# A mixer's second output projection by a seven-product scheme, behind each two gate pairs

## The chip, the cores and the metric

The kernel runs on one core of one Trainium2 chip. The metric is the device time of one execution in microseconds (us): the median of several runs. Engines are named as the profile names them: PE is TensorE (matmuls), PEld its weight loads, DVE is VectorE, ACT is ScalarE, POOL is GpSimd, SP is SyncE, which here only issues transfers.

## The reference

Two layers (DEPTH = 2) of a streaming encoder, on 640 tokens: 512 of a new stream and 8 x 16 of running streams. Everything is float32.

```python
x += 1/2 * SwiGLU_1(RMSNorm(x))
h  = RMSNorm(x)
z  = h @ w_in              # conv B | conv C | conv V | q | k | v | gates
y_conv = B * causal_depthwise_conv3(C * V)          # 512 channels
y_attn = chunk-band attention, 8 heads x 64         # 512 channels
g_conv, g_attn = split(sigmoid(gates + b_gate))     # 1024 columns each
m  = g_conv * (y_conv @ w_conv_out) + g_attn * (y_attn @ w_attn_out)
x += m @ w_o
x += 1/2 * SwiGLU_2(RMSNorm(x))
```

`w_conv_out` and `w_attn_out` are 512 x 1024, `w_o` is 1024 x 1024.

## The kernel before

**Layout.** Channels lie on the 128 partitions, the 640 tokens (T) along the free dimension, in two halves of 320 (HT, called t1 and t2). A row of 1024 outputs is KT = 8 tiles of 128; the inputs of `w_attn_out` are CT = 4 tiles.

**Precision.** Each float32 operand is split into a high part (a rounded copy, made by ScalarE, L306 for weights) and a low part (operand minus high part, made by VectorE, L311). A product is three matmuls: high x high, high weight x low input, low weight x high input (`multiply`, `block`).

**Weights** come from one stream in HBM in transfers of 128 x 1024 (`raw`, three buffers, issued by SP at L246). A slab is what one step of TensorE uses; `prep` casts it and leaves its low part in `pending`, `flush` makes the low parts. `slab(True)` hands out the next slab, after it has put the cast of the slab two further on into ScalarE's order. The high and low parts have three buffers each.

**By seven.** Some products are done as a 2 x 2 block product with seven block products in place of eight (Winograd's form of Strassen's scheme). Tokens are cut into halves and inputs into even and odd tiles. A group of output tiles needs sums of weights (VectorE, L250, four half-slabs a group), sums of inputs (made once), and seven blocks of 12 matmuls of 320 columns, in four slabs: slab 0 gives blocks one and two, slab 1 three and four, slab 2 five and six, slab 3 the seventh. Several blocks add onto one PSUM bank; between them the bank's content is copied out, since the intermediate values are needed too.

**The output stage** (`outputs`, in each layer after attention) has its order written out by hand: PE, DVE and ACT run their instructions strictly in the order in which the program gives them. It goes through:

- `gate_pair(m)` for m = 2 to 14, two gate tiles at a time, by seven over the normalised input `h` (called g2, g4, ... here). It has banks pa, pb and pc. In pairs 2, 4 and 6 the intermediate products are copied to SBUF (L1300) and added by POOL's accumulating transfers (`accumulate`, L1280); in pairs 8 to 14, marked `direct`, VectorE adds them from PSUM (`take`).
- `unit(m0, to)` for m0 = 0 and 4: four output tiles of `w_conv_out` by seven, over the input sums `xhi`/`xlo` made of `yc`. Banks A, B and two of C.
- `out(m)`, two after each of pairs 8 to 14: one output tile of `w_attn_out` as a plain product (`product`, L373): 4 input tiles x 3 matmuls x 2 halves. The parts of `yas`, the attention's output, are made by `taken` (L1483) and `took` (L1490). Then the product is multiplied with its gate (L1468) and added to `mm`.
- Small pieces of VectorE's and ScalarE's work are put at four spots of each pair or unit with `at(place, spot, job)`: `scale` (times the norm's factors, L1283), `bend` (two sigmoids, L1125), `weigh` (`mm` times its gate).
- `give` splits the merged rows `mm` into the operands `mo` of `w_o` (L220, L221), most of them during the last two `out`s.

Then `mixer` does the eight rows of `w_o`, one after the other, each a plain product over the eight operands (bank `po`), adds each to `x` (L1206) and prepares the next block's inputs.

Of the kernel before, what the change touches and what calls it, by code (L numbers as in the profile page):

```python
# [108 lines left out]
def mixer_order():  # L109

    mix = lambda *rows: ("mix", rows)
    out = [("v", None)] + [mix(("q", p), ("k", p)) for p in range(AW // P)]
    for c in range(0, CT, 2):
        out += [mix(("C", c + i), ("V", c + i)) for i in range(2)] + [mix(("B", c), ("B", c + 1))]
    gates = [mix(("g", m), ("g", m + 1)) for m in range(0, 2 * KT, 2)]
    out += gates[:4] + [("unit", ("co", 0)), ("unit", ("co", 4))]
    for i, g in enumerate(gates[4:]):
        out += [g, ("ao", 2 * i), ("ao", 2 * i + 1)]  # L120
    return out + [("o", m) for m in range(KT)]


# [58 lines left out]
def trunk(ctx: ExitStack, tc: tile.TileContext, xin, wst, small, pbias, samplebias, kcache, vcache,  # L182
# [24 lines left out]
    def acc(name):  # L207
        return banks["acc"].tile([P, 2, 512], F32, tag="acc", name=name)
# [40 lines left out]
    def add(out, a, b):  # L249
        DVE.tensor_tensor(out=out, in0=a, in1=b, op=ALU.add)  # L250
# [135 lines left out]
    def product(ps, ops, at=()):  # L386
        for _ in steps(ps, ops, at):
            pass
# [718 lines left out]
    def mixer(l, after):  # L1107
# [91 lines left out]
        ex = after()  # L1199
        with tc.manual_schedule(engines=ORDERED):  # L1200
            hold[0] = True
            for m in range(KT):
                po = acc(f"po{l}_{m}")
                product(po, mo)
                ex.weights(m)
                DVE.tensor_tensor(out=halves(x[m]), in0=two(po), in1=halves(x[m]), op=ALU.add)  # L1206
                if m < KT - 1:
                    flush()
                ex.final(m)
# [51 lines left out]
    def outputs(l, gp, X, st, cs, yc, yas, sigmoid, gates):  # L1261
# [20 lines left out]
        def times(out, g):  # L1282
            DVE.tensor_tensor(out=out, in0=out, in1=g, op=ALU.mult)  # L1283

        def gate_pair(m):
            n = f"{l}_{m}"
            pa, pb, pc = (att(f"q{i}{n}")[:, :HT] for i in "abc")
            direct = m >= KT
            if m in (4, 6):
                u, g = (gp.tile([P, T], F32, name=f"g{n}{i}") for i in "ab")  # L1290
            else:
                u, g = tmp(f"g{n}"), tmp(f"g{n}_1")
            gates[m], gates[m + 1] = u, g
            me = f"g{m}"

            def take(out, ps, c):
                if direct:
                    add(out, ps, out)
                else:
                    ACT.copy(c, ps)  # L1300
                    accumulate(out, c)

            s0 = quiet()
            block(pa, s0, 0, x11, every, True, True)
            ACT.copy(u[:, t1], pa)
            prep(used[0] + 1)
            flush()
            spot(me, 1)
            block(pb, s0, 1, x21, every, True, True)
            if direct:  # L1310
                take(u[:, t1], pb, cs[0])
# [9 lines left out]
            if not direct:  # L1321
                take(u[:, t1], pb, cs[0])
# [7 lines left out]
            if direct:  # L1330
                times(g[:, t2], rr[:, t2])
                times(u, rr)
                sigmoid(u, m)
            block(pa, s3, 0, xT4, every, False, True)
            DVE.tensor_tensor(out=g[:, t1], in0=pa, in1=rr[:, t1], op=ALU.mult)
            if direct:
                sigmoid(g, m + 1, -1.0)
            flush()
            spot(me, 4)

# [6 lines left out]
        def bend(m):  # L1347
            def job():
# [1 line left out]
                sigmoid(gates[m + 1], m + 1, -1.0)  # L1350
            return job

        v = yc.rearrange("p (i o) (t c) -> p i o t c", o=2, t=2)
# [3 lines left out]
        vs = [v[:, i].rearrange("p o t c -> p (o t) c") for i in range(2)]  # L1357

        def high(i, c, z):
            ACT.copy(xhi[:, i, c], z)  # L1360
# [1 line left out]
        def low(i, c, z):  # L1362
            DVE.tensor_tensor(out=xlo[:, i, c], in0=z, in1=xhi[:, i, c].bitcast(F32), op=ALU.subtract)

        def opening():
            high(slice(0, 2), 4, v[:, :, 0, 0])
            for i in range(2):
                high(i, slice(5, 7), v[:, i, 1])

        def firsts():  # L1370
            low(slice(0, 2), 4, v[:, :, 0, 0])
            DVE.tensor_tensor(out=v[:, :, 0, 0], in0=v[:, :, 0, 0], in1=v[:, :, 0, 1], op=ALU.subtract)

        def lasts():
            DVE.tensor_tensor(out=v[:, :, 0, 1], in0=v[:, :, 1, 1], in1=v[:, :, 0, 1], op=ALU.subtract)
            for a, b in ((v[:, :, 0, 0], v[:, :, 1, 1]), (v[:, :, 1, 1], v[:, :, 1, 0])):
                DVE.scalar_tensor_tensor(out=b, in0=a, scalar=-1.0, in1=b, op0=ALU.mult, op1=ALU.subtract)

        def raw_low(i):
            return lambda: low(i, slice(5, 7), v[:, i, 1])  # L1380

        def sum_high(i):
            return lambda: high(i, slice(0, 4), vs[i])

        def sum_low(i):
            return lambda: low(i, slice(0, 4), vs[i])

        def unit(m0, to):

            n = f"{l}_{m0}"  # L1390
            A, B = (acc(f"{i}co{n}") for i in ("ba" if m0 else "ab"))
            if m0:
                A, B = B, A
            C = [att(f"c{i}co{n}")[:, :HT] for i in range(2)]
            a, b = ([z[:, i, :HT] for i in range(2)] for z in (A, B))
            me = f"c{m0}"

            def mul(ps, s, half, kind, start):
                for i in range(2):
# [51 lines left out]
                    times(mm[m], gates[m])  # L1451
            return job

        def parts(pool, tag, name, src):
            hi, lo = (pool.tile([P, T], F32R, tag=f"{tag}{i}", name=f"{name}{i}") for i in ("hi", "lo"))
            split(hi, lo, src)
            return hi, lo

        ya, mo = [], []

        def out(m, then=None):

            py = acc(f"py{l}_{m}")
            product(py, ya)
            if then:
                then()
            g = gates[m + KT]
            DVE.tensor_tensor(out=halves(g), in0=two(py), in1=halves(g), op=ALU.mult)  # L1468
            add(mm[m], mm[m], g)
            flush()  # L1470

        def give(ms):
            for m in ms:
                mo.append(parts(hp, "h", f"m{l}_{m}", mm[m]))

        for c in range(CT):
            ya.append(tuple(z[:, c // 2, :].rearrange("p a b -> p (a b)")[:, (c % 2) * T : (c % 2 + 1) * T]
                            for z in (xhi, xlo)))

        def taken(*cs):  # L1480
            def job():
                for c in cs:
                    ACT.copy(ya[c][0], yas[:, c, :])  # L1483
            return job

        def took(*cs):
            def job():
                for c in cs:
                    hi, lo = ya[c]
                    DVE.tensor_tensor(out=lo, in0=yas[:, c, :], in1=hi.bitcast(F32), op=ALU.subtract)  # L1490
            return job

        at("g2", 1, opening)
        at("g2", 2, firsts)
        at("g2", 3, raw_low(0))
        at("g2", 4, raw_low(1))
        at("g4", 1, lasts)
        at("g4", 3, sum_high(0))
        at("g4", 4, sum_high(1))
        at("g6", 1, sum_low(0))  # L1500
        at("g6", 2, sum_low(1))
        at("g6", 3, scale(2))
        at("g6", 4, bend(2))
        at("c0", 1, scale(4))
        at("c0", 2, bend(4))
        at("c0", 3, scale(6))
        at("c0", 4, bend(6))
        at("c4", 2, weigh(0, 1))
        at("c4", 4, weigh(2, 3))
        at(f"g{KT}", 1, taken(0, 1))  # L1510
        at(f"g{KT}", 2, took(0, 1), taken(2, 3))
        at(f"g{KT}", 3, took(2, 3))
        at(f"g{KT + 2}", 2, weigh(5, 7))
        at(f"g{KT + 2}", 4, weigh(4, 6))
        for m in (2, 4, 6):
            gate_pair(m)
        unit(0, yc)
        unit(CT, spare)
# [566 lines left out]
```

## Time and profile before

| | |
|---|---|
| median of 3 runs | 2506.02 us (2505.72 to 2506.08) |
| profiled execution | 2506.0 us, span from first to last instruction 2504.2 us |
| PE busy | 2486.0 us, 99% of the span, 17096 matmuls |
| DVE busy | 2104.6 us, 84% |
| ACT busy | 1420.0 us, 57% |
| POOL busy | 335.6 us, 13% |
| mean granted TensorE clock | 0.998 of full |
| transfers | 299.59 MB, mean 120 GB/s |

Busy time of PE counts pipelined matmuls from start to end; what bounds a stage is read from the starts. A row of the timeline has the start, the duration, the engine, the line, the operation, output<-inputs by the program's names, shapes and a count; in square brackets stands the idle time before it and who ended it. Rows of groups have the count, the busy time and the mean duration.

### The profile page before, as it was taken

To read this page: it belongs to the slowest core of one execution; us is meant where nothing else is said; L and a number is where in the kernel's file an instruction comes from. 1 tells how busy PE (TensorE), PEld (TensorE's weight loads), DVE (VectorE), ACT (ScalarE), POOL (GpSimd) and SP (SyncE) were. 2 spreads that over 40 slices of the span, in tenths; PEclk is the share of its full clock that TensorE was granted. 3 is DMA by queue.
4 is the path that set the end of the run, shared out by engine and by line. 5 is a ranking of instruction groups with operands and counts; after the bars stand their busy time and mean duration, and the time that the engine had idled before them with its cause. 6 is when DMAs were issued, how large, how long until landed. Compare 5 with 4: busy or idle time off the path is not lost. (4 is left out here: it accounts for less than half of the span.)

```text
span 2504.2 us, 43427 instructions
## 1 busy us (share of the span) xinstructions
PE 2486.0 (99%) x17096; PEld 2427.1 (97%) x17096; DVE 2104.6 (84%) x3304; ACT 1420.0 (57%) x2281; POOL 335.6 (13%) x407
## 2 busy tenths in 40 slices
PE   9999999999999999999999999999999999999998
PEld 8999999888999999999999999998899999999998
DVE  7888888878886899888788889888788868989887
ACT  7455556665654555555555555556646455555554
POOL 0011211211100011111002111221111000111111
PEclk9999999999999999999999999999999999999999
DMA  4245665335423444656435565643444243455554
GB/s 145 81 110 123 138 137 130 108 105 173 108 73 107 101 116 116 137 134 135 116 87 128 129 133 122 137 119 117 133 143 108 77 114 94 119 132 120 131 135 110
DMA packets 127021, 299.59 MB, mean 120 GB/s; under 512 B 12160, under 2 KB 70912, under 8 KB 126816
## 3 DMA queue, kind: packets, MB, share of 16 engines
q1 hardware_dynamic: 68976, 219.18, 27.6%
q0 software_dynamic: 57120, 76.98, 18.4%
q8 instruction: 134, 2.20, 0.4%
q10 hardware_dynamic: 720, 0.65, 0.1%
q14 instruction: 71, 0.58, 0.1%
HBM read 221.13 MB, written 7.94 MB: 91 GB/s over the span
## 5 line engine op out<-in xcount | busy, mean ns | idle before, releaser
L311 DVE TENSOR_TENSOR wlo<-raw,whi 128x1024 fp32r<-128x1024 f32 (+1 forms) x575 | 593.8, 1035 | 224.3 <-ACT whi L306 218.9
L306 ACT CAST whi<-raw 128x1024 fp32r<-128x1024 f32 (+1 forms) x575 | 516.0, 902 | 362.7 <-PE pbb L396 44.3
L306 ACT CAST whi<-s 128x1024 fp32r<-128x1024 f32 (+1 forms) x160 | 151.2, 945 | 249.5 <-issue 114.4
L396 PE MATMUL pab<-xhib,whi 128*128 128x320 f32 x704 | 218.2, 310 | 0.6 <-ACT ub L813 0.6
L396 PE MATMUL pab<-xhib,wlo 128*128 128x320 f32 x704 | 217.5, 309 | 0.8 <-DVE wlo L311 0.8
L396 PE MATMUL pab<-xlob,whi 128*128 128x320 f32 x704 | 217.3, 309 | 0.0
L396 PE MATMUL paa<-xhia,whi 128*128 128x320 f32 x640 | 198.0, 309 | 0.3 <-ACT ua L813 0.3
L396 PE MATMUL paa<-xhia,wlo 128*128 128x320 f32 x640 | 197.7, 309 | 0.4 <-DVE wlo L311 0.4
L396 PE MATMUL paa<-xloa,whi 128*128 128x320 f32 x640 | 197.7, 309 | 0.1
L311 DVE TENSOR_TENSOR wlo<-s,whi 128x1024 fp32r<-128x1024 f32 (+1 forms) x160 | 174.1, 1088 | 12.7 <-ACT whi L306 12.7
L396 PEld LDWEIGHTS pab<-xhib,wlo 128*128 128x128 f32 x704 | 132.1, 188 | 1.3 <-DVE wlo L311 1.3
L396 PEld LDWEIGHTS pab<-xhib,whi 128*128 128x128 f32 x704 | 132.2, 188 | 1.3 <-ACT ub L813 1.1
L396 PEld LDWEIGHTS pab<-xlob,whi 128*128 128x128 f32 x704 | 132.2, 188 | 0.2
L396 PEld LDWEIGHTS paa<-xhia,wlo 128*128 128x128 f32 x640 | 120.1, 188 | 0.7 <-DVE wlo L311 0.7
L396 PEld LDWEIGHTS paa<-xhia,whi 128*128 128x128 f32 x640 | 120.2, 188 | 0.6 <-ACT ua L813 0.6
L396 PEld LDWEIGHTS paa<-xloa,whi 128*128 128x128 f32 x640 | 120.2, 188 | 0.4 <-DVE xloa L555 0.4
L250 DVE TENSOR_TENSOR raw<-raw,raw 128x512 f32<-128x512 f32 x160 | 109.4, 684 | 1.4
L250 DVE TENSOR_TENSOR raw<-s,raw 128x512 f32<-128x512 f32 x160 | 109.8, 686 | 0.0
L396 PE MATMUL pcb<-xhib,whi 128*128 128x320 f32 x352 | 108.9, 309 | 0.4 <-ACT gb L832 0.4
L396 PE MATMUL pcb<-xhib,wlo 128*128 128x320 f32 x352 | 108.8, 309 | 0.0
L396 PE MATMUL pcb<-xlob,whi 128*128 128x320 f32 x352 | 108.6, 309 | 0.0
L979 POOL DMA_DIRECT2D x<-c_b x52 | 62.6, 1204 | 310.6 <-ACT c_b L972 134.8
(703 smaller groups left out, 8077.2 us busy)
## 6 DMA issues: line engine op xcount, KB each, us to landing
raw<-in_wst SPq DMA_DIRECT2D x375, 512.0 KB, 3.9
x<-c_b POOLq DMA_DIRECT2D x52, 320.0 KB, 5.0
x<-c_a POOLq DMA_DIRECT2D x50, 320.0 KB, 5.0
kc<-in_kcache SPq DMA_DIRECT2D x32, 256.0 KB, 3.9
vc<-in_vcache SPq DMA_DIRECT2D x16, 512.0 KB, 4.8
ub<-cbb POOLq DMA_DIRECT2D x42, 160.0 KB, 5.3
ua<-cba POOLq DMA_DIRECT2D x38, 160.0 KB, 5.2
x<-u_a POOLq DMA_DIRECT2D x18, 320.0 KB, 5.1
```

The lines of the kernel that those rows point to most:

```text
L250: DVE.tensor_tensor(out=out, in0=a, in1=b, op=ALU.add)
L306: ACT.copy(hi[:, d], src[:, c])
L311: DVE.tensor_tensor(out=lo, in0=src, in1=hi.bitcast(F32), op=ALU.subtract)
L396: PE.matmul(ps, a, b, start=start and kp == 0 and j == 0, stop=stop and kp == NP - 1 and j == 2, skip_group_check=True)
L979: POOL.dma_start(rows(r, cols), z, accum_op=ALU.add)
```

## The change

1. `w_attn_out` is done by seven as `w_conv_out` is: two units (`ao`, 0 and 4) in place of eight plain rows. They stand behind each two gate pairs: 8, 10, unit, 12, 14, unit. The host lays its weights out accordingly.
2. The sums of the attention's output that a unit needs are made in `yas` itself, in steps at spots of gate pairs 8 and 10 (class `Inputs`, used for both inputs now). The first unit writes its result over `yas`, the second into `held`, the buffer of gates 4 to 7.
3. Gate pairs 8 to 14 take the way of 2 to 6: copies by ScalarE and accumulating transfers by POOL, no `direct`.
4. Gating and merging become jobs: `join` (result times gate, added to `mm`), `give` (high part) and `gave` (low part).
5. The first two rows of `w_o` are done together, by inputs in the order 0, 1; 2, 3; 4, 6; 5, 7: both rows for each two inputs.

```diff
-    for i, g in enumerate(gates[4:]):
-        out += [g, ("ao", 2 * i), ("ao", 2 * i + 1)]
+    out += gates[4:6] + [("unit", ("ao", 0))] + gates[6:] + [("unit", ("ao", 4))]
...
+            pos = [acc(f"po{l}_{m}") for m in range(2)]
+            ws = [[tiles.take() for _ in range(KT)] for _ in pos]
+            for ks in ((0, 1), (2, 3), (4, 6), (5, 7)):
+                for po, w in zip(pos, ws):
+                    for k in ks:
+                        multiply(po, w[k], mo[k], k == 0, k == KT - 1)
             for m in range(KT):
-                po = acc(f"po{l}_{m}")
-                product(po, mo)
+                if m < len(pos):
+                    po = pos[m]
+                else:
+                    po = acc(f"po{l}_{m}")
+                    product(po, [mo[k] for k in range(KT)])
...
+        held = gp.tile([P, CT, T], F32, name=f"gt{l}")
...
             def take(out, ps, c):
-                if direct:
-                    add(out, ps, out)
-                else:
-                    ACT.copy(c, ps)
-                    accumulate(out, c)
+                ACT.copy(c, ps)
+                accumulate(out, c)
...
+        class Inputs:
+            def opening(self):
+                high(slice(0, 2), 4, self.v[:, :, 0, 0])
+                for i in range(2):
+                    high(i, slice(5, 7), self.v[:, i, 1])
+            def firsts(self):
+                v = self.v
+                low(slice(0, 2), 4, v[:, :, 0, 0])
+                DVE.tensor_tensor(out=v[:, :, 0, 0], in0=v[:, :, 0, 0], in1=v[:, :, 0, 1], op=ALU.subtract)
+            def lasts(self):
+                v = self.v
+                DVE.tensor_tensor(out=v[:, :, 0, 1], in0=v[:, :, 1, 1], in1=v[:, :, 0, 1], op=ALU.subtract)
+                for a, b in ((v[:, :, 0, 0], v[:, :, 1, 1]), (v[:, :, 1, 1], v[:, :, 1, 0])):
+                    DVE.scalar_tensor_tensor(out=b, in0=a, scalar=-1.0, in1=b, op0=ALU.mult, op1=ALU.subtract)
...
+        def join(*ms):
             def job():
+                for m in ms:
+                    times(ya[m], gates[KT + m])
+                    add(mm[m], mm[m], ya[m])
...
+        def give(*ms):
+            def job():
+                for m in ms:
+                    mo[m] = tuple(hp.tile([P, T], F32R, tag=f"h{i}", name=f"m{l}_{m}{i}") for i in ("hi", "lo"))
+                    ACT.copy(mo[m][0], mm[m])
...
+        def gave(*ms):
+            def job():
+                for m in ms:
+                    hi, lo = mo[m]
+                    DVE.tensor_tensor(out=lo, in0=mm[m], in1=hi.bitcast(F32), op=ALU.subtract)
...
-        at(f"g{KT}", 1, taken(0, 1))
-        at(f"g{KT}", 2, took(0, 1), taken(2, 3))
-        at(f"g{KT}", 3, took(2, 3))
-        at(f"g{KT + 2}", 2, weigh(5, 7))
-        at(f"g{KT + 2}", 4, weigh(4, 6))
+        at("g8", 1, second.opening)
+        at("g8", 2, second.firsts)
+        at("g8", 3, second.raw_low(0))
+        at("g8", 4, second.raw_low(1), second.lasts)
+        at("g10", 1, second.sum_high(0))
+        at("g10", 2, second.sum_high(1), second.sum_low(0))
+        at("g10", 3, second.sum_low(1))
+        at("g10", 4, scale(8))
+        at("ao0", 1, bend(8))
+        at("ao0", 2, scale(10))
+        at("ao0", 3, bend(10))
+        at("ao0", 4, join(0))
+        at("g12", 1, join(1))
+        at("g12", 2, join(2))
+        at("g12", 3, join(3))
+        at("g14", 1, scale(12))
+        at("g14", 2, bend(12), weigh(4, 5))
+        at("g14", 3, weigh(6, 7))
+        at("ao4", 1, give(0, 1))
+        at("ao4", 2, gave(0, 1))
+        at("ao4", 3, scale(14), give(2, 3))
+        at("ao4", 4, bend(14), gave(2, 3))
...
-        for m in range(0, KT, 2):
-            gate_pair(m + KT)
-            last = m == KT - 2
-            out(m, (lambda: give(range(3))) if last else None)
-            out(m + 1, (lambda: give(range(3, 6))) if last else None)
-        give(range(6, KT))
+        for m in (8, 10):
+            gate_pair(m)
+        unit("ao", 0, yas)
+        for m in (12, 14):
+            gate_pair(m)
+        unit("ao", CT, held)
+        for i, m in enumerate((4, 6, 5, 7)):
+            join(m)()
+            give(m)()
+            if i:
+                gave(was)()
+            was = m
+        gave(was)()
```

More of the change, by code (lines that the diff above doesn't have):

```diff
@@ L1287, in gate_pair @@
             pa, pb, pc = (att(f"q{i}{n}")[:, :HT] for i in "abc")
-            direct = m >= KT
             if m in (4, 6):
-                u, g = (gp.tile([P, T], F32, name=f"g{n}{i}") for i in "ab")
+                u, g = held[:, m - 4], held[:, m - 3]
             else:
@@ L1309, in gate_pair @@
             block(pb, s0, 1, x21, every, True, True)
-            if direct:
-                take(u[:, t1], pb, cs[0])
             s1 = slab(True)[0]
@@ L1320, in gate_pair @@
             spot(me, 3)
-            if not direct:
-                take(u[:, t1], pb, cs[0])
+            take(u[:, t1], pb, cs[0])
             block(pa, s2, 0, xT7, every, False, True)
@@ L1329, in gate_pair @@
             s3 = slab(True)[0]
[L1330 to L1333, printed above, removed]
             block(pa, s3, 0, xT4, every, False, True)
             DVE.tensor_tensor(out=g[:, t1], in0=pa, in1=rr[:, t1], op=ALU.mult)
-            if direct:
-                sigmoid(g, m + 1, -1.0)
             flush()
@@ L1351, in bend @@
             return job
-        v = yc.rearrange("p (i o) (t c) -> p i o t c", o=2, t=2)
         xhi, xlo = (gp.tile([P, 2, 7, HT], F32R, name=f"x{i}{l}") for i in ("hi", "lo"))
@@ L1356, in outputs @@
                  for i in range(2)]
-        vs = [v[:, i].rearrange("p o t c -> p (o t) c") for i in range(2)]
         def high(i, c, z):
@@ L1363, in low @@
             DVE.tensor_tensor(out=xlo[:, i, c], in0=z, in1=xhi[:, i, c].bitcast(F32), op=ALU.subtract)
[L1365 to L1391, printed above, removed]
+        class Inputs:
+            def __init__(self, y):
+                self.v = y.rearrange("p (i o) (t c) -> p i o t c", o=2, t=2)
+                self.vs = [self.v[:, i].rearrange("p o t c -> p (o t) c") for i in range(2)]
+            def opening(self):
[11 more added lines that the diff above has]
+                    DVE.scalar_tensor_tensor(out=b, in0=a, scalar=-1.0, in1=b, op0=ALU.mult, op1=ALU.subtract)
+            def raw_low(self, i):
+                return lambda: low(i, slice(5, 7), self.v[:, i, 1])
+            def sum_high(self, i):
+                return lambda: high(i, slice(0, 4), self.vs[i])
+            def sum_low(self, i):
+                return lambda: low(i, slice(0, 4), self.vs[i])
@@ L1392, in unit @@
+        def unit(name, m0, to):
+            n = f"{name}{l}_{m0}"
+            A, B = (acc(f"{i}{n}") for i in ("ba" if m0 else "ab"))
             if m0:
                 A, B = B, A
-            C = [att(f"c{i}co{n}")[:, :HT] for i in range(2)]
+            C = [att(f"c{i}{n}")[:, :HT] for i in range(2)]
             a, b = ([z[:, i, :HT] for i in range(2)] for z in (A, B))
-            me = f"c{m0}"
+            me = f"{name}{m0}"
             def mul(ps, s, half, kind, start):
@@ L1452, in weigh @@
             return job
[L1454 to L1480, printed above, removed]
+        def join(*ms):
             def job():
-                for c in cs:
-                    ACT.copy(ya[c][0], yas[:, c, :])
-            return job
-        def took(*cs):
+                for m in ms:
+                    times(ya[m], gates[KT + m])
+                    add(mm[m], mm[m], ya[m])
+            return job
@@ L1487, in job @@
+        mo = {}
+        def give(*ms):
             def job():
-                for c in cs:
-                    hi, lo = ya[c]
-                    DVE.tensor_tensor(out=lo, in0=yas[:, c, :], in1=hi.bitcast(F32), op=ALU.subtract)
-            return job
[L1493 to L1500, printed above, removed]
@@ L1501, in outputs @@
-        at("g6", 2, sum_low(1))
+                for m in ms:
+                    mo[m] = tuple(hp.tile([P, T], F32R, tag=f"h{i}", name=f"m{l}_{m}{i}") for i in ("hi", "lo"))
+                    ACT.copy(mo[m][0], mm[m])
+            return job
+        def gave(*ms):
[3 more added lines that the diff above has]
+                    DVE.tensor_tensor(out=lo, in0=mm[m], in1=hi.bitcast(F32), op=ALU.subtract)
+            return job
+        ya = [z[:, i] for z in (yas, held) for i in range(CT)]
@@ L1502, in outputs @@
+        first, second = Inputs(yc), Inputs(yas)
+        at("g2", 1, first.opening)
+        at("g2", 2, first.firsts)
+        at("g2", 3, first.raw_low(0))
+        at("g2", 4, first.raw_low(1))
+        at("g4", 1, first.lasts)
+        at("g4", 3, first.sum_high(0))
+        at("g4", 4, first.sum_high(1))
+        at("g6", 1, first.sum_low(0))
+        at("g6", 2, first.sum_low(1))
         at("g6", 3, scale(2))
         at("g6", 4, bend(2))
-        at("c0", 1, scale(4))
-        at("c0", 2, bend(4))
@@ L1506, in outputs @@
[L1506 to L1509, printed above, removed]
-        at(f"g{KT}", 1, taken(0, 1))
-        at(f"g{KT}", 2, took(0, 1), taken(2, 3))
-        at(f"g{KT}", 3, took(2, 3))
-        at(f"g{KT + 2}", 2, weigh(5, 7))
-        at(f"g{KT + 2}", 4, weigh(4, 6))
+        at("co0", 1, scale(4))
+        at("co0", 2, bend(4))
+        at("co0", 3, scale(6))
+        at("co0", 4, bend(6))
+        at("co4", 2, weigh(0, 1))
+        at("co4", 4, weigh(2, 3))
@@ L1515, in outputs @@
+        at("g12", 2, join(2))
[7 more added lines that the diff above has]
+        at("ao4", 4, bend(14), gave(2, 3))
         for m in (2, 4, 6):
             gate_pair(m)
-        unit(0, yc)
-        unit(CT, spare)
-        for m in range(0, KT, 2):
-            gate_pair(m + KT)
-            last = m == KT - 2
-            out(m, (lambda: give(range(3))) if last else None)
-            out(m + 1, (lambda: give(range(3, 6))) if last else None)
@@ L1524, in outputs @@
-        give(range(6, KT))
+        unit("co", 0, yc)
+        unit("co", CT, spare)
+        for m in (8, 10):
[11 more added lines that the diff above has]
+        gave(was)()
         assert not jobs
```

## The prediction

> **What bounds the kernel now.** I read the page first, then the windows of the mixer's output stage, then the rows of TensorE, VectorE and ScalarE in it.
>
> ```profile
> span 2504.2 us, 43427 instructions
> PE 2486.0 (99%) x17096; PEld 2427.1 (97%) x17096; DVE 2104.6 (84%) x3304; ACT 1420.0 (57%) x2281; POOL 335.6 (13%) x407
> ...
> 704.80:782.30 77.50, 77.50 (x530) 77.50 (x530) 62.98 (x90) 37.34 (x56) 0.00 (x0) 1.00 0.27 89
> 1943.40:2020.90 77.50, 77.50 (x530) 77.50 (x529) 62.98 (x91) 37.32 (x56) 0.00 (x0) 1.00 0.27 89
> ```
>
> TensorE is busy for 99% of the span, so only fewer matmuls make the kernel faster, and every wait put before a matmul makes it slower. The two windows (length, then the busy time of PE, its weight loads, DVE, ACT and POOL, the granted clock, the share of the DMA engines and GB/s) are the stage that the change rewrites, from gate pair 8 to the first row of w_o, once in each layer. They are alike to 0.02 us, so I work out layer 0 and take it twice. TensorE never stops there, and VectorE has 14.5 us to spare.
>
> ```profile
> 704.78 0.30 PE L396 MATMUL qa<-hhim,whi 128*128 128x320 f32 x1
> ...
> 717.12 0.46 PE L373 MATMUL py<-xhi,whi 128*128 128x320 f32 x2
> ...
> L373 PE MATMUL py<-xhi,whi 128*128 128x320 f32 x128 | 29.1, 309 | 0.0
> ...
> L373 PE MATMUL py<-xhi,wlo 128*128 128x320 f32 x128 | 29.1, 309 | 0.0
> ```
>
> Gate pair 8 is 84 matmuls in 717.12 - 704.78 = 12.34 us: 0.1469 us each, start to start (the 309 ns are pipelined). A block of 12 takes 1.763 us.
>
> **What is removed.** The plain product has three groups of 128 in two layers (the first and the last are shown): 384 matmuls. By seven, each unit has 7 products x 12 = 84, so 4 units have 336. 48 go: 48 x 0.1469 = 7.05 us, or 3.53 us a layer. All of it lies on TensorE's path. The Trainium skill (TensorE: Matmul & The Clock Gate, Back-to-back issue gap) gives N / 2.4 + 2.5 ns for a warm matmul, 135.8 ns at 320 columns; by it 6.5 us would go, and the measured 146.9 ns decides.
>
> **What is added.** The stage now is g8, g10, ao0, g12, g14, ao4: six groups of 84, 74.0 us. From the program's order, VectorE has in it 39 operations on 512 columns, 13 on 1024, 2 on 1280, 32 on 640 and 12 on 320. By the spacings below that is 69.3 us of 74.0, or 94%. ScalarE goes from 55 operations to 81. Neither is a bound on average. But both run strictly in written order, and TensorE waits on them for more than weights: products are added onto banks that hold earlier ones, and TensorE may not write a bank again until ScalarE has copied it out. The trace already shows how such a copy comes late:
>
> ```profile
> 691.24 0.69 DVE L250 TENSOR_TENSOR s<-raw,raw 128x512 f32<-128x512 f32 x1
> ...
> 692.04 0.62 ACT L306 CAST whi<-s 128x512 fp32r<-128x512 f32 x1 [2.21 <-PE aco L1405]
> 692.57 0.62 ACT L306 CAST whi<-raw 128x512 fp32r<-128x512 f32 x1
> 693.10 0.70 ACT L1412 ACTIVATE yc<-aco 128x640 f32<-128x640 f32 x1
> ...
> 693.46 0.30 PE L1405 MATMUL aco<-xhi,wlo 128*128 128x320 f32 x1
> 693.84 0.41 PE L1405 MATMUL bco<-xhi,whi 128*128 128x320 f32 x1
> 694.10 0.31 PE L1405 MATMUL bco<-xlo,whi 128*128 128x320 f32 x1
> ```
>
> VectorE's half-sum ends at 691.93, the casts queue behind it, the copy of the bank queues behind the casts and ends at 693.80, and TensorE resumes at 693.84: 0.23 us late, and another 0.11 us at the second matmul. I look for the places where the new order does this, walking the queues with these spacings:
>
> ```profile
> 709.11 1.22 DVE L311 TENSOR_TENSOR wlo<-raw,whi 128x1024 fp32r<-128x1024 f32 x1
> 710.25 0.48 DVE L250 TENSOR_TENSOR g<-qb,g 128x320 f32<-128x320 f32 x1
> 710.65 0.68 DVE L311 TENSOR_TENSOR wlo<-raw,whi 128x512 fp32r<-128x512 f32 x1
> 711.25 3.03 DVE L1490 TENSOR_TENSOR xlo<-ya,xhi 128x640 fp32r<-128x640 f32 x4
> ...
> 660.38 0.82 DVE L1375 TENSOR_TENSOR yc<-yc 128x640 f32<-128x640 f32 x1
> 661.23 1.68 DVE L1377 SCALAR_TENSOR_TENSOR yc<-yc 128x640 f32<-128x640 f32 x2
> 662.83 0.69 DVE L311 TENSOR_TENSOR wlo<-raw,whi 128x512 fp32r<-128x512 f32 x1
> ...
> 672.00 1.49 DVE L1363 TENSOR_TENSOR xlo<-yc,xhi 128x1280 fp32r<-128x1280 f32 x1
> 673.40 0.68 DVE L311 TENSOR_TENSOR wlo<-raw,whi 128x512 fp32r<-128x512 f32 x1
> ...
> 707.06 1.05 ACT L306 CAST whi<-raw 128x1024 fp32r<-128x1024 f32 x1
> 708.01 1.35 ACT L1483 CAST xhi<-ya 128x640 fp32r<-128x640 f32 x2
> ...
> 663.36 1.27 ACT L1360 CAST xhi<-yc 128x1280 fp32r<-128x1280 f32 x1
> 664.52 0.42 ACT L1300 COPY capsm<-qb 128x320 f32<-128x320 f32 x1
> ...
> 686.08 0.83 ACT L1125 ACTIVATE g_4a<-g_4a,sm 128x640 f32<-128x640 f32 x1 [0.37 <-DVE g_4a L1283]
> 686.82 0.82 ACT L1125 ACTIVATE g_4b<-g_4b,sm 128x640 f32<-128x640 f32 x1
> ...
> 717.31 0.49 DVE L1335 TENSOR_TENSOR g<-qa,rrm 128x320 f32<-128x320 f32 x1
> ```
>
> VectorE, start to start: 1024 columns 1.14, 512 0.60, 640 0.735 (0.85 where the next needs its result), 320 0.40, 1280 1.40; three half-sums together 2.04. ScalarE: 1024 0.95, 512 0.53, 640 0.63, 1280 1.16, a sigmoid 0.73; a copy of 640 columns is through after 0.70, one of 320 after 0.43.
>
> *A, fifth block of g10.* At 717.31 VectorE does what it does now, the scaling of g8's last block, 0.41. Then: two 512 (1.21), the raw low part (0.735), the three differences of the attention inputs (0.85 + 1.60), and g10's half-sum for slab 2 (through after 0.69): 722.80. ScalarE: cast of slab 2 to 723.75, sum_high(0) to 724.91, cast of 512 to 725.44, and only then the copy, 725.87. TensorE wants the bank at 717.12 + 4 x 1.763 = 724.17 and starts 0.04 after the copy: 1.74 late.
>
> *B, fifth block of ao0.* TensorE reaches it at 725.91 + 7 x 1.763 = 738.25. VectorE from 725.53, where the cast of 512 ends: 512, two low parts of 1280, a 1024, half-sums, 320, two 512, scale(8), the half-sum for slab 2: 735.53. ScalarE: 0.95 + 0.53, bend(8)'s two sigmoids 1.46, the copy 0.70: 739.17. 0.96 late.
>
> *C, seventh block of ao0.* Wanted at 742.74. The copy stands behind bend(10)'s sigmoids, which wait for scale(10), done at 740.19 or so: they start after the cast at 740.65, and the copy ends at 742.81. 0.11 late.
>
> *D, third block of g12.* Its u now lies in the buffer of gate 8, so the copy waits for join(0)'s product, which VectorE reaches after ao0's additions, ending at 748.09; the copy ends at 748.55. Wanted at 748.14: 0.45 late.
>
> *E, sixth block of g14.* The copy of pc stands behind bend(12), which waits for scale(12), which stands behind three joins (1.60 each) and slab 2's low part. It ends at 766.4, wanted at 766.22: 0.25 late.
>
> *F, fifth block of ao4.* After four weighings (2.94), a 1024, half-sums, 320, two 512 and the half-sum, VectorE is at 773.85. Casts 0.95 + 0.53, give(0, 1) 1.25, copy 0.70: 777.28, wanted at 777.03: 0.30 late.
>
> *G, w_o.* Let E be the end of ao4. VectorE then has, in its order from E + 0.1: the low part of a w_o slab 1.13, two gave 1.47, join(4)'s product 0.74, another slab 1.16 (its buffer comes free only with ao4's last block), and additions, products and low parts up to gave(6), 0.74 + 0.85 + 0.73 + 0.73 + 0.85 + 0.74, through after 0.82: E + 10.1. Interleaved rows give TensorE eight operand steps of inputs 0 to 3 (7.05 us), then input 4 (0.88), then it wants the low part of 6 at E + 8.2: 1.85 late. Inputs 5 and 7 come in time.
>
> Sum: 5.66 us. Each walk passes some hand-overs of 0.03 to 0.11 us that I left out (ACT after DVE above: 691.93 to 692.04); 0.08 at each of seven places makes 6.2. What goes is the wait that w_o has now:
>
> ```profile
> 787.58 0.46 PE L373 MATMUL po<-m_6hi,whi 128*128 128x320 f32 x2
> 788.12 0.56 PE L373 MATMUL po<-m_6lo,whi 128*128 128x320 f32 x2
> 788.51 0.31 PE L373 MATMUL po<-m_6hi,wlo 128*128 128x320 f32 x1
> ```
>
> Two matmuls take 0.29, so 0.25 is lost before 788.12 and 0.10 after it. A layer: 6.2 - 0.35 - 3.53 = +2.3 us; two layers +4.6. The profiled execution took 2506.0 (span 2504.2), the median of the runs is 2506.02: **2510.6 us**.
>
> **What is moved past the queues.** The gates now add three banks each through POOL's accumulating transfers instead of VectorE: 12 more a layer.
>
> ```profile
> raw<-in_wst SPq DMA_DIRECT2D x3, 512.0 KB, 4.3
> ...
> g_6b<-c POOLq DMA_DIRECT2D x1, 160.0 KB, 4.7
> ```
>
> POOL does nothing else in the stage. The last transfer of a gate pair is issued as its sixth block ends, and the scale that needs it comes 7 us later or more: at 4.7 us to landing this costs nothing (cover: 2 us). SP's weight loads are as many as before, but a load starts when VectorE gives a buffer back, which is now later. g12's second load is issued at about 737.8 and needed at 741.9: 4.1 us against the 4.3 above. Here I count nothing.
>
> **Rivals.**
> *The weights become the wait* (slower still). If landings grow from 4.3 to 5.0 beside the 12 added transfers, g12's half-sum starts 0.9 later, and g10's, whose margin is like it, 0.6: 1.5 us a layer, all in VectorE's chain, 2513.6. Against: the load share was only 0.27. 0.17.
> *The cover holds everywhere* (the other side). If each copy came in time, 2506.0 - 7.05 = 2499.0. It decides at A: the new order would have to reach the copy 1.7 us earlier, and no spacing above is off by that. 0.06.
> *Half of it holds.* If A and B vanish because VectorE runs ahead there, 2.7 us a layer go: 2505.2. 0.07.
> *A stall slows the clock.* This row pair speaks of it:
>
> ```profile
> 847.94 1.17 PE L473 MATMUL npsb<-ones,ssumb 128*128 128x1 f32 x10
> 848.97 0.39 PE L396 MATMUL pab<-xhib,whi 128*128 128x320 f32 x1
> 849.20 0.31 PE L396 MATMUL pab<-xlob,whi 128*128 128x320 f32 x1
> 849.35 0.31 PE L396 MATMUL pab<-xhib,wlo 128*128 128x320 f32 x1
> ```
>
> After 1.03 us with next to no work TensorE is back at 0.15 us from the second matmul on. If each stall of 1.7 us or more, A and G, made the two blocks after it (24 matmuls) take double, it would cost 3.5 us more, 14 us in all: 2524.6. The Trainium skill (the same page, HAM oscillation) puts the threshold at idle gaps over about 3.4 us; by that rule it does not happen here. 0.02.
>
> **How the numbers follow.** The forecast gets 0.68. Its own range, stalls of 4.7 to 7.4 us a layer, is 2507.6 to 2513.0. The range of 2506.5 to 2516.0 holds that and late weights, over 8 in 10. About 0.2%, or 5.0 us, is what I count as a difference: the line is at 2511.0, just above the forecast, so it splits 0.37 within to 0.31 slower. Slower: 0.31 + 0.17 + 0.02 = 0.50. Within: 0.37 + 0.07 = 0.44. Faster: 0.06.
>
> **What would show it.** TensorE's waits list ScalarE's copies before g10's fifth block (L1319's copy, 1.5 to 2 us), ao0's fifth block (about 1 us), and VectorE's low part of input 6 before w_o (1.4 us or more), in both layers; the stage from gate pair 8 to w_o takes 77 to 79 us instead of 77.5. It is wrong if that stage takes under 76 us, if the waits name the weights' loads, or if w_o starts without a stop.

## The result, and the profile after

The changed kernel takes 2511.18 us (median of 15 runs, 2510.49 to 2511.73). The kernel before takes 2505.84 us beside it (15 runs, 2505.43 to 2507.67). The ratio is 1.002, with a 95% interval of 1.0013 to 1.0027: 5.3 us slower, where 4.6 were forecast, and the median lies 0.6 us above the forecast. The interval runs from 3.3 to 6.8 us, so it does not settle on which side of the prediction's line of 5.0 us the change falls; the median is 0.3 us beyond it. The profiled execution took 2511.28 us, with a span of 2509.5 us.

The first line of the page says what became of the saving, and the windows of the rewritten stage (length, busy time of PE, its weight loads, DVE, ACT and POOL, then clock and transfers) say where the rest came from:

```profile
PE 2482.4 (99%) x17048; PEld 2419.7 (96%) x17048; DVE 2130.8 (85%) x3334; ACT 1449.8 (58%) x2343; POOL 356.6 (14%) x431
```

```profile
705.04:783.50 78.46, 75.42 (x506) 74.01 (x505) 70.92 (x100) 48.56 (x81) 10.50 (x12) 1.00 0.41 107
1946.30:2024.75 78.45, 75.41 (x506) 74.00 (x505) 70.91 (x99) 48.49 (x82) 10.48 (x12) 1.00 0.40 109
```

The 48 matmuls are gone (17096 to 17048). The stage from gate pair 8 to w_o takes 78.46 us in place of 77.50, in both layers alike, and TensorE, which never stopped in it, is now idle for 3.04 us of it (by the starts of its matmuls it loses more, 4.5 us; see the seven stalls below). The rest of its stops lies in w_o. The list of TensorE's waits over the whole run (total, times, longest) names the places, each twice, once a layer:

```profile
PE qa L395 <- ACT g L1319: 3.3, 2, 1.7
PE po L372 <- DVE m_6lo L1478: 2.4, 2, 1.2
PE aao L1409 <- ACT ya L1416: 1.6, 2, 0.8
...
PE qa L395 <- ACT g L1311: 0.7, 2, 0.3
```

The largest, the fifth block of g10 (called A in the prediction), looks like this in the timeline of DVE, ACT and PE:

```profile
720.77 1.69 DVE L1381 SCALAR_TENSOR_TENSOR ya<-ya 128x640 f32<-128x640 f32 x2
722.37 0.68 DVE L249 TENSOR_TENSOR raw<-s,raw 128x512 f32<-128x512 f32 x1
...
723.14 1.05 ACT L305 CAST whi<-raw 128x1024 fp32r<-128x1024 f32 x1 [3.38 <-DVE raw L249]
724.10 1.25 ACT L1355 CAST xhi<-ya 128x1280 fp32r<-128x1280 f32 x1
725.25 0.61 ACT L305 CAST whi<-raw 128x512 fp32r<-128x512 f32 x1
725.77 0.42 ACT L1319 COPY g<-qa 128x320 f32<-128x320 f32 x1
...
726.24 0.42 PE L395 MATMUL qa<-thi,whi 128*128 128x320 f32 x1 [1.66 <-ACT g L1319]
726.50 0.31 PE L395 MATMUL qa<-tlo,whi 128*128 128x320 f32 x1
```

VectorE works off the input differences up to 722.4, its half-sum follows, ScalarE, idle until then, casts that half-sum, an input sum and another 512 columns of weights, and only then copies the bank, until 726.19. TensorE has waited 1.66 us. And at w_o (G):

```profile
791.85 0.45 PE L372 MATMUL po<-m_6hi,whi 128*128 128x320 f32 x2
793.47 0.57 PE L372 MATMUL po<-m_6lo,whi 128*128 128x320 f32 x2 [1.17 <-DVE m_6lo L1478]
793.89 0.46 PE L372 MATMUL po<-m_6hi,wlo 128*128 128x320 f32 x2
```

Two matmuls take 0.29 us, so 1.33 is lost before 793.47 and 0.13 behind it.

### The profile page after: what moved, and what is told of

Same layout as the page of the kernel before. It is cut to its first block, busy times and chain, and to the rows that moved or that the text cites. A ratio compares the mean times of both kernels' runs of the same rounds, so it can differ in the third digit from the quotient of the medians.

```text
span 2509.5 us, 43502 instructions
## 1 busy us (share of the span) xinstructions
PE 2482.4 (99%) x17048; PEld 2419.7 (96%) x17048; DVE 2130.8 (85%) x3334; ACT 1449.8 (58%) x2343; POOL 356.6 (14%) x431
## 5 line engine op out<-in xcount | busy, mean ns | idle before, releaser
L310 DVE TENSOR_TENSOR wlo<-raw,whi 128x512 fp32r<-128x512 f32 (+1 forms) x583 | 598.6, 1030 | 230.2 <-ACT whi L305 224.9
L305 ACT CAST whi<-raw 128x512 fp32r<-128x512 f32 (+1 forms) x583 | 520.0, 897 | 363.8 <-PE pbb L395 44.3
```

Source lines behind the costliest of these rows:

```text
L305: ACT.copy(hi[:, d], src[:, c])
L310: DVE.tensor_tensor(out=lo, in0=src, in1=hi.bitcast(F32), op=ALU.subtract)
```

## The experiments

The times per place had come out as forecast, but that leaves open why they are what they are. Two theories were set against each other.

*Local order*: each stall is made at its own place, by what happens to stand ahead of one copy; move that, and the stall goes. This is how the prediction reads them, one by one.

*The relay*: VectorE as a whole is full in this stage. Its waits tell it, before and after, in the 80 us from 704 to 784, each list with its window:

```profile
DVE g L250 <- PE qa L396: 7.4, 3, 3.2
DVE wlo L311 <- ACT whi L306: 3.5, 3, 1.2
...
DVE g L1468 <- PE py L373: 1.1, 2, 0.6
```

```profile
DVE wlo L310 <- ACT whi L305: 6.4, 8, 1.2
DVE g L1334 <- PE qa L395: 0.6, 1, 0.6
```

```profile
704.00:784.00 80.00, 76.96 (x517) 75.55 (x516) 72.46 (x102) 49.88 (x83) 10.50 (x12) 1.00 0.41 108
```

Before, VectorE waited 8.5 us for TensorE's banks (7.4 + 1.1): that is slack. After, 0.6 of it is left. It is busy for 72.46 us, and for 6.4 us it waits for ScalarE's casts of the weights: 78.9 of 80. Its last wait for TensorE is at 717.57, before A; from there to the last low part of w_o it has none. Those waits for casts are the relay. A half-sum of weights (VectorE) goes to a cast (ScalarE) and back to a low part (VectorE), and where the order has nothing between half-sum and low part, VectorE stands still for one cast:

```profile
761.39 0.68 DVE L249 TENSOR_TENSOR raw<-s,raw 128x512 f32<-128x512 f32 x1
...
762.16 1.57 ACT L305 CAST whi<-raw 128x1024 fp32r<-128x1024 f32 x2 [1.31 <-DVE raw L249]
...
763.24 1.22 DVE L310 TENSOR_TENSOR wlo<-raw,whi 128x1024 fp32r<-128x1024 f32 x1 [1.17 <-ACT whi L305]
764.38 1.22 DVE L1291 TENSOR_TENSOR g<-g,rrm 128x640 f32<-128x640 f32 x2
```

By this theory only VectorE's work or its idle time counts, and a stall that is moved comes back further on. The median of before measured beside each of the runs below is 2505.74 or 2505.88 us.

### ScalarE's copies earlier, VectorE's work as it is

```diff
-        at("ao0", 1, bend(8))
-        at("ao0", 2, scale(10))
-        at("ao0", 3, bend(10))
+        at("ao0", 2, bend(8), scale(10))
+        at("ao0", 4, bend(10))
...
-        at("g14", 2, bend(12), weigh(4, 5))
-        at("g14", 3, weigh(6, 7))
-        at("ao4", 1, give(0, 1))
+        at("g14", 2, weigh(4, 5))
+        at("g14", 3, bend(12), weigh(6, 7))
+        at("ao4", 2, give(0, 1))
```

> ScalarE's order alone: bend(8) and bend(10) in the first attention unit, bend(12) in gate pair 14 and give(0, 1) in the second unit each go one spot later, behind the copy of the bank that they stood in front of. Theory of local order (the prediction's): each late copy has its own cause, so the stalls at ao0's fifth and seventh block (1.06 and 0.11), g14's sixth (0.38) and ao4's fifth (0.40) go: 1.95 us a layer, 2507.3 us. Rival, the relay: VectorE and ScalarE hand slab 2 to each other (half-sum, cast, low part) and VectorE's queue is nearly full, so the time is lost in the chain as a whole; a stall taken away at one place comes back at the next (g12's third block, w_o). It says 2511.2, within 0.6.

Measured: 2511.59 us (2510.93 to 2512.51), ratio 1.0023 [1.0014, 1.0032]. The stall of ao0's fifth block (ya) is gone from TensorE's waits, and the third block of g12 (g L1311) waits 1.5 us in place of 0.3:

```profile
PE qa L395 <- ACT g L1319: 1.7, 1, 1.7
PE qa L395 <- ACT g L1311: 1.5, 1, 1.5
PE po L372 <- DVE m_6lo L1478: 1.2, 1, 1.2
PE po L372 <- ACT gt L1416: 0.4, 1, 0.4
```

The sigmoids (at ao4's fifth block, the casts of `give`) were what stood ahead of those copies, as the prediction had it, but taking them out of the way gained nothing. TensorE resumes at A and at w_o here:

```profile
727.42 0.42 PE L395 MATMUL qa<-thi,whi 128*128 128x320 f32 x1 [1.66 <-ACT g L1319]
...
794.68 0.56 PE L372 MATMUL po<-m_6lo,whi 128*128 128x320 f32 x2 [1.20 <-DVE m_6lo L1478]
```

That is 67.26 us, and 726.24 to 793.47 in the changed kernel is 67.23. TensorE comes earlier to g12, because the stalls in ao0 are gone, and waits there for the same work of VectorE until the same moment; what it gains behind that it loses at w_o. This speaks for the relay, and against reading the stalls as separate losses.

### An input sum later

```diff
-        at("g10", 1, second.sum_high(0))
-        at("g10", 2, second.sum_high(1), second.sum_low(0))
-        at("g10", 3, second.sum_low(1))
-        at("g10", 4, scale(8))
+        at("g10", 2, second.sum_high(0))
+        at("g10", 3, second.sum_high(1), second.sum_low(0))
+        at("g10", 4, second.sum_low(1), scale(8))
```

> The casts of the attention's input sums in gate pair 10 go one spot later: sum_high(0) behind the copy that was late at the fifth block, sum_high(1) to spot 3, the low parts behind them. Local order: the stall there falls by the 1.16 us of that cast, 2508.9 us in all. Relay: the half-sum of slab 2 still comes when it came, the low parts now run into the first unit, and what is saved at g10 comes back at ao0 and g12: 2511.6, within 0.6.

Measured: 2511.8 us (2511.39 to 2512.21), ratio 1.0024 [1.0014, 1.0033]. TensorE's waits in layer 0:

```profile
PE aao L1409 <- ACT ya L1416: 1.3, 2, 0.8
...
PE qa L395 <- ACT g L1319: 0.5, 1, 0.5
PE qa L395 <- ACT g L1311: 0.3, 1, 0.3
PE qa L395 <- ACT c L1306: 0.3, 1, 0.3
```

A fell from 1.7 to 0.5 by taking one cast of 1280 columns from ahead of the copy. New waits stand behind it (0.3 in g10, another 0.5 in ao0), and the time is no better. The local order had it 2.3 us faster. VectorE's own waits hardly changed in sum: 5.9 us for casts of weights in place of 6.4, but 0.2 for the cast of an input sum and 0.4 for a transfer of weights, which it does not wait for in the changed kernel. This run alone does not separate the theories: the moved casts and low parts now stand ahead of other copies, which would make new local stalls too.

### Less work for VectorE

```diff
-        at("g8", 4, second.raw_low(1), second.lasts)
+        at("g8", 4, second.raw_low(1))
```

> Leaves out the three differences of the attention's inputs (one subtraction and two reversed subtractions of 640 columns, 2.45 us of VectorE behind gate pair 8), so the sums that the units use are not formed. Theory of local order: they are the cause of the stall at g10's fifth block, so 1.93 us a layer go there and the later stalls stay: 2507.3. Relay: VectorE's chain is 2.45 us shorter and nothing behind it makes up for it: the stall at g10 goes whole, that at ao0's fifth block by half, 2506.3. A rival that these operations lie beside TensorE's work (they took 2.4 us of a stage with 5 us to spare) says 2511.2.

Measured: 2506.06 us (2505.72 to 2507.48), ratio 1.0001 [0.9993, 1.001]. What was taken from VectorE is 2.45 us a layer (0.85 and 1.60 by the prediction's spacings); what the kernel gained on the changed one is 5.12 us, 2.56 a layer. So the work taken from VectorE here came off the kernel's time in full. The two theories lie only 1.0 us apart (2507.3 and 2506.3), and the interval reaches about 2 us to either side, so the trace has to decide. TensorE's waits in layer 0 no longer show A, and ao0's fifth block waits 0.3 in place of 0.8, which the local order had left as it was:

```profile
PE qa L395 <- ACT g L1311: 0.3, 1, 0.3
PE aao L1409 <- ACT ya L1416: 0.3, 1, 0.3
```

### Less idle time for VectorE

The job of spot 1 is put between the half-sum and its low part, in `gate_pair` and in `unit`:

```diff
-            flush()
             spot(me, 1)
+            flush()
```

> One swap in the order of VectorE, in gate pairs and units: the job of spot 1 now stands between the half-sum of slab 2 and its low part, so VectorE has work while ScalarE casts. No operation is added or taken away and ScalarE's order stays as it is but for jobs of its own at that spot. The relay theory says that the 1.2 us for which VectorE waits for the cast go wherever the job at spot 1 has work for VectorE (co0, g12, g14, and the ends behind them): about 1.9 us a layer, 2507.4 us, with the stalls at g10 and ao0 left as they are, since their jobs at spot 1 are ScalarE's. The theory of local order says that the copies stand behind the same instructions as before: 2511.2.

Measured: 2507.67 us (2507.56 to 2508.33), ratio 1.0007 [0.9999, 1.0016]: 3.5 us below the changed kernel. At the place shown above, the product with the norm's factors now fills the cast's time, and no idle time is left in front of the low part:

```profile
759.94 0.69 DVE L249 TENSOR_TENSOR raw<-s,raw 128x512 f32<-128x512 f32 x1
760.54 1.22 DVE L1291 TENSOR_TENSOR g<-g,rrm 128x640 f32<-128x640 f32 x2
761.80 1.83 DVE L310 TENSOR_TENSOR wlo<-raw,whi 128x1024 fp32r<-128x1024 f32 x2
```

VectorE's waits from 704 to 784 have the sum of it:

```profile
DVE wlo L310 <- ACT whi L305: 4.6, 6, 1.2
```

It is 6.4 - 4.6 = 1.8 us a layer less. That twice this is near the 3.5 us gained is partly chance. By the starts of its matmuls TensorE lost 7.0 us from 676 to 805 in the changed kernel and loses 5.3 here: 0.5 us less in the second unit of `w_conv_out`, 0.4 at E, 0.3 at F and 0.5 at w_o. The first of these lies ahead of 704, where VectorE's waits for casts are 3.6 us in both kernels; behind 704 the gain is 1.2 us a layer for 1.8 us less of waiting, and VectorE now waits 0.4 us for a bank of ao4. No work was taken away, and ScalarE's order is the same: filling VectorE's idle time shortened the stage behind A. Only at E could the local order claim as much, since scale(12) now runs ahead of the low part that it stood behind. The same two lines swapped in the kernel before, whose VectorE has slack:

> The kernel before with the same swap alone (job of spot 1 between the half-sum of slab 2 and its low part, in pairs and units). Relay: the two small stalls of its second convolution unit (0.61 us a layer) go, with nothing else to gain: 2504.6 us. Otherwise 2505.8.

Measured: 2504.68 us (2504.22 to 2506.57), ratio 0.9996 [0.9988, 1.0005], by the times not to be told from no change. The trace shows that the two stalls of the convolution unit are gone (0.60 us before, 0.10 now, layer 0), so about 1 us of the 3.5 above has nothing to do with the attention's units.

### The transfers of POOL

```diff
-                accumulate(out, c)
+                if m < KT:
+                    accumulate(out, c)
```

> Leaves out the accumulating transfers of gate pairs 8 to 14, three a pair, so those gates lack a part of their sums; ScalarE's copies stay. My theory says that these transfers hide: their landing is waited for by no one long, and 2511.2 us stay, within 0.4. A rival, that they hold up the weight loads or VectorE's scale jobs, says 2509 or less.

Measured: 2511.68 us (2511.14 to 2512.26), ratio 1.0023 [1.0014, 1.0032]. That is 0.5 us above the changed kernel, just outside the 0.4 expected, and on the side away from the rival. The added transfers are hidden, as counted.

### The rows of w_o one after another

```diff
-            pos = [acc(f"po{l}_{m}") for m in range(2)]
-            ws = [[tiles.take() for _ in range(KT)] for _ in pos]
-            for ks in ((0, 1), (2, 3), (4, 6), (5, 7)):
-                for po, w in zip(pos, ws):
-                    for k in ks:
-                        multiply(po, w[k], mo[k], k == 0, k == KT - 1)
+            pos = []
```

> The change without its last part: the first two rows of w_o come one after the other again, inputs 0 to 7 in turn. My theory says that the interleaving is cover: row 0 alone reaches input 4 after 3.5 us, while VectorE delivers the low part of input 4 about 7.5 us after the last unit and those of 5 and 7 about 12 and 13 us after it. TensorE then loses about 6.7 us at w_o in place of 1.9: 4.8 us a layer, 2520.8 us. A rival, that the parts come in time for one row as well, says 2511.2 as with the interleaving.

Measured: 2524.95 us (2524.42 to 2525.38), ratio 1.0076 [1.0063, 1.0089]: 13.8 us above the changed kernel, and 4.15 more than expected. The interleaving covers what it should: up to its last stop there, TensorE's starts put 6.7 us of loss at w_o in each layer (1.5, 1.3, 0.1, 1.7, 2.0 and 0.1 in layer 0), as expected. The surplus is in the clock (windows, granted clock third from the right), in both layers:

```profile
787.00:790.00 3.00, 0.73 (x3) 0.46 (x4) 2.97 (x5) 1.45 (x2) 0.00 (x0) 1.00 0.05 20
790.00:793.00 3.00, 1.50 (x6) 0.94 (x6) 2.93 (x5) 0.73 (x1) 0.00 (x0) 0.87 0.00 0
793.00:796.00 3.00, 1.59 (x7) 1.50 (x7) 2.27 (x3) 0.72 (x1) 0.00 (x0) 0.50 0.00 0
796.00:799.00 3.00, 3.00 (x13) 3.00 (x13) 0.00 (x0) 0.00 (x0) 0.00 (x0) 0.50 0.51 175
799.00:802.00 3.00, 3.00 (x22) 3.00 (x21) 2.43 (x3) 1.46 (x2) 0.00 (x0) 0.99 0.00 0
```

```profile
2038.00:2039.00 1.00, 0.94 (x4) 0.54 (x3) 0.97 (x2) 0.00 (x0) 0.00 (x0) 0.54 0.00 0
...
2048.00:2049.00 1.00, 1.00 (x8) 1.00 (x7) 1.00 (x1) 1.00 (x2) 0.00 (x0) 0.84 0.00 0
```

The clock is at half for about 6.8 us in layer 0 and 10.2 us in layer 1, if a mean between 0.50 and 1.00 is read as a share of its window. The timeline of TensorE shows the pace that this means, and the waits ahead of it:

```profile
788.26 0.57 PE L372 MATMUL po<-m_4hi,whi 128*128 128x320 f32 x2 [1.35 <-ACT m_4hi L1466]
...
792.19 0.90 PE L372 MATMUL po<-m_5hi,whi 128*128 128x320 f32 x2 [1.50 <-ACT m_5hi L1466]
794.50 0.90 PE L372 MATMUL po<-m_5lo,whi 128*128 128x320 f32 x2 [1.41 <-DVE m_5lo L1473]
...
795.73 0.73 PE L372 MATMUL po<-m_6hi,whi 128*128 128x320 f32 x2
796.26 0.73 PE L372 MATMUL po<-m_6lo,whi 128*128 128x320 f32 x2
```

Two matmuls take 0.53 us in place of 0.29. TensorE is back at work without a stop from 794.5 on, so 4.6 us are spent at half pace in layer 0 and, from 2042.4 on, 5.9 us in layer 1. At 1 - 0.294 / 0.53 = 0.445 that is 10.5 x 0.445 = 4.7 us lost, an estimate 0.5 us above the 4.15 not expected. (In the waits before 794.5 the half clock costs next to nothing, since TensorE waits for VectorE anyway.)

### A version with the relay filled

The two lines swapped as above; `second.lasts` from g8's spot 4 to g10's spot 1; both high sums at g10's spot 2, both low sums at spot 3; `scale(8)` to ao0's spot 1; `bend(8)` to ao0's spot 3, `bend(10)` to its spot 4, `bend(12)` to g14's spot 3; `join(0)` to a new spot between the additions of C and the next; and single inputs in w_o:

```diff
-            for ks in ((0, 1), (2, 3), (4, 6), (5, 7)):
+            for ks in ((0, 1), (2, 3), (4,), (6,), (5,), (7,)):
...
                 add(rows(0, t2)[:, i], C[i], rows(0, t2)[:, i])
+            spot(me, 5)
```

> The change with the relay filled: the swap of e6; the three differences moved to spot 1 of g10, so that they fill the wait for the cast; both casts of the sums to spot 2 and their low parts to spot 3; scale(8) and the sigmoids behind the copies; join(0) right after the row that it needs; and inputs 4, 6, 5, 7 of w_o one at a time for both rows. All operations are those of the change. By the relay theory about 1.6 us a layer of stalls stay (0.2 at ao0, 0.3 at g14, 1.1 at w_o) against the 0.96 of the kernel before: 2506.0 - 7.05 + 2 x 0.65 = 2500.2 us. If the nearly full queue itself is the bound and not the order of what stands in it, it stays above 2506.

Measured: 2501.7 us (2501.25 to 2502.0), ratio 0.9983 [0.9974, 0.9991]: 9.5 us below the changed kernel and 4.2 below the one before, though 1.5 above what was expected. From 704 to 784 VectorE waits for casts for 1.9 us in place of 6.4, and TensorE is busy for all but 0.03 us:

```profile
DVE wlo L310 <- ACT whi L305: 1.9, 3, 1.2
```

```profile
704.00:784.00 80.00, 79.97 (x542) 79.26 (x541) 76.64 (x107) 53.20 (x87) 10.51 (x12) 1.00 0.42 117
```

By the starts, TensorE loses 2.2 us from 676 to 805 in place of 7.0. Of the 4.8 us a layer, 3.8 are at A to F, 0.5 in the second unit of `w_conv_out` (the swap again) and 0.5 at w_o, where the single inputs were not tried alone. The moves at A to F were made together as well, so what each is worth is not shown. VectorE is busy for 76.64 of the 80 us and TensorE loses 0.7 us in them: VectorE's nearly full queue was not the bound by itself, the order in it was. What is left of TensorE's waits is in w_o:

```profile
PE po L372 <- DVE m_5lo L1479: 0.3, 1, 0.3
PE po L372 <- DVE m_6lo L1479: 0.2, 1, 0.2
```

It has the same 17048 matmuls as the changed kernel. So the saving of seven products is real, and it was the order of VectorE's and ScalarE's work that ate it. By the trace, about 1 us of the 4.2 below the kernel before is the swap's, which that kernel can have too (2504.68 above).

## Why the prediction was right, and where its reading was not

**The saving.** 48 matmuls went, as counted, and they were on TensorE's path: the last version, with the stalls mostly gone, is 4.2 us faster than before, and 2.7 above the 2499.0 that the prediction gives if the cover holds everywhere.

**The seven stalls.** All seven stand at the places named. The sizes are close, one sign apart: w_o's wait for the low part of input 6 was to be 1.4 us or more and is 1.17. From the starts of the matmuls, the second one's delay in it, A has 1.93 us, B 1.06, C 0.11, D 0.59, E 0.38, F 0.40, and G, in three pieces, 1.9: about 6.4 us a layer, where 6.2 were forecast. That the sum is so near is in part luck. The late starts alone make 5.4 us, where the walks had 5.66: G's 1.85 came out as 1.33 before input 6's low part and 0.20 before input 4's, where no stop was forecast. Against that, the 0.08 a place for hand-overs, 0.56 in all, stands against about 1.0 us of second matmuls, 0.10 to 0.13 after each stop, which the prediction had seen once and did not count at its places. (C's 0.11 was forecast for the first matmul and came at the second.) From the first input matmul of `w_conv_out`'s units to the first one behind w_o a layer took 2.45 us longer (forecast 2.3): 4.9 of the 5.3. Of the remaining 0.4 us, 0.3 lies ahead of those units: TensorE's first matmul of them starts at 679.79 in place of 679.52, and its waits list a stop of 0.4 us in the first 60 us (poa, for a low part) that the kernel before does not have. The same stop comes and goes among the runs above, so it is not laid to the change.

**POOL and the weights.** Nothing was counted for them, and the run without the transfers is 0.5 us slower than the changed kernel, not faster. No wait for weights shows in the stage after: the rival of late weights did not occur.

**The reading that fell short** is in the part on what is added: "69.3 us of 74.0, or 94% ... Neither is a bound on average." As an average it stands: the last version does the same operations, and TensorE loses 0.7 us in the 80 from 704 to 784. But the 69.3 us leave out the time in which VectorE stands and waits for a cast. With the 6.4 us of the relay it is 75.7 us, more than the 74.0 that TensorE needs, so in the order written VectorE was the bound of the stage behind A. (This sum does not give the size of the loss: the stage took 78.46 us, with VectorE busy for 70.92 of them.) The 14.5 us "to spare" before were not all spare either: 3.5 of them were such waits. The walks from place to place had those hand-overs in them, which is why the numbers held. But taken as seven separate losses they suggest wrong cures: the two runs that moved ScalarE's part or the casts in front of one copy gained nothing. For the same reason the rival "half of it holds", 2505.2 with A and B gone, is not likely to come about by an order that spares these two alone, though no run tried it; the run that did take A away, and half of B, at 2506.06, had taken 2.45 us of work out of VectorE.

**The clock rival.** It gave 2524.6 if stalls of 1.7 us slowed the clock. In the changed kernel the granted clock is 1.00 throughout the stage and w_o, after the stop of 1.66 us as after that of 1.17: right to discard it there. The reason for it was too weak, as the run with w_o's rows in turn shows (below).

**The range** held the result. Its forecast case, stalls of 4.7 to 7.4 us a layer, is what occurred.

## What to carry to other kernels

Where an engine does both ends of a hand-over (half-sum, then low part) and another does the middle, add the middle's time to the first engine's load unless something stands between: here 94% of work and 6.4 us of such waits made VectorE the bound. A stall at TensorE names the instruction that came last, not the engine that is full; before you move that instruction, look whether the feeding engine still has waits for TensorE in its own list (8.5 us before, 0.6 after), since without such slack a moved stall comes back. Work that can wait belongs between the two ends of the hand-over. Here the new order as a whole was worth 9.5 us, more than the 7.05 of the removed matmuls.

## What the runs showed of the hardware

**The clock halves without a long stop.** In the run with the rows in turn, no wait of TensorE in the stretch is listed above 1.50 us, but from 787 to 790 it was busy for 0.73 of 3.00 us and from 790 to 793 for 1.50. Within the second of these the clock fell to 0.50, and it stayed there until TensorE had worked without a stop for 4.6 us, in layer 1 for 5.9. In the changed kernel single stops of 1.66 and 1.17 us, with full work around them, cost no clock. The Trainium skill (TensorE: Matmul & The Clock Gate, HAM oscillation) speaks of idle gaps over about 3.4 us; the measurement goes against taking that as the only condition. The Trainium skill (the same page, A second HAM failure mode: psum-queue depth-cycling) tells of frequent micro-idles that make the clock swing, and this trace agrees in so far as the clock fell with short stops alone; it fell once a layer and did not swing. Which of length, number or share of the stops decides is not shown here.

**A stop costs 0.10 to 0.13 us more than its wait.** After each of A to G the second matmul starts that much late, as 726.24 to 726.50 shows for A: 0.26 in place of 0.147. The cause is not shown.
